# Attention scores as three fp32r products in place of one f32 product, in a whole two-block model

## The chip, the cores and the metric

The kernel runs on one core of one Trainium2 chip: TensorE (PE in the profile) multiplies, its weight loads are listed apart as PEld; VectorE (DVE), ScalarE (ACT) and GpSimd (POOL) do the rest, and SyncE (SP) issues most transfers. The metric is device time in microseconds (us) for one execution. Engines run their own instructions in order, and wait for each other by semaphores.

## The reference, cut to what matters

One batch of 512 tokens, 1024 wide, goes through two blocks. Block one: a hybrid attention (8 heads of a sparse kind with three branches: compressed keys, selected keys, a window; 8 heads of a block kind), then a mixture of 32 experts. Block two: a convolution of 31 taps beside a forgetting attention of 16 heads, then a layer that gathers experts (PEER). All is f32. With 512 tokens, the selections cover all visible keys, so that each branch is a causal softmax with a bias.

```python
qn = rms_norm(_heads(q_n, NSA_HEADS), nsa_q_gain)          # 8 heads of 64
kc = rms_norm(_compress(k_cmp, ...), k_gain)               # 31 compressed keys
ks, kw = rms_norm(k_slc, k_gain), rms_norm(k_win, k_gain)  # 2 groups of 64
s = einsum("bghcd,bgcmd->bghcm", qn, ks) * scale - sl * dist   # selected; window alike
o = gates[0] * softmax(s_cmp) @ vc + gates[1] * softmax(s_slc) @ vs + gates[2] * softmax(s_win) @ vw
# 8 heads of the block kind
qm, km = rms_norm(_heads(q_m, 8), moba_q_gain), rms_norm(_heads(k_m, 8), moba_k_gain)
o = softmax(qm @ km.T * scale - sl * dist) @ vm
# block two, forgetting attention; c = cumsum(log_sigmoid(f))
s = einsum("bhqd,bhkd->bhqk", q, k) / 8 + c[..., :, None] - c[:, :, None, :]
o = softmax(where(causal, s, NEG_2)) @ v
```

## The kernel before

Activations lie transposed, features on partitions. A value that goes into a wide product is kept as two fp32r parts, the high part a rounded copy and the low part what is left (`split`, L121 to L128: ACT copies, DVE subtracts), and a product is three matmuls, high by high, high by low, low by high (`mm3`, L130). Weights come in chunks of 128 columns through `stream` (L184): SP loads them into three raw buffers, ACT makes `sh` (L202), and DVE, or in the second attention POOL (`self.low`), makes `sl` (L203), two chunks ahead of use. The attention scores alone are f32 matmuls of 64 rows by head (`attend`, L986).

`attend` (L972 to L1055) runs both attentions. A unit is a pair of heads, a block of 128 queries and all keys up to it, 128 to 512. The first attention has 48 units (per head pair j four query blocks by two branches: 32 units; then four pairs of the block kind: 16), the second 32 (eight pairs by four blocks). Turn t issues, in this order: the two heads' scores of unit t (L986, with the forget term L988 added in the second attention), the maximum on DVE (`aw`, L1000) and the exponential on ACT (`ap`, L1003); the division of unit t-1 (one head on ACT, one on DVE, L1009 to L1017); the transposes of unit t-2 (L1025) with copies (`apt`, L1029 DVE, L1031 ACT); the products with values of t-3 (L1040). Each head has one bank of scores.

Between two turns the caller puts work that doesn't belong to the unit. In the first attention: one entry of the list `self.later`, then a chunk of the projection, eight steps of `mm3` in PSUM bank `acc`. Chunks come in the order key, query, value of each pair, numbered from 0 (0 and 1 are `vs`, `vw`). A finished query or key chunk goes through `head_norm` (L240): ACT writes the square and a copy times -0.5 at once (L247, L248); the rest, put on `self.later`, is a matmul that sums the squares by head (L252), three steps on ACT (Ln, Exp, Square: L254, L255, L258) and three on DVE (L259, L260, L261, the last writes the normalised heads `qn`, `qm`, `km`). A finished value chunk is copied by ACT (`vT`, L232) and later turned. The list is emptied in full (`flush`) ahead of units 0, 8, 16, 24, 32, 36, 40 and 44, where a new head pair begins and DVE makes its two bias tables (`bias`, L599).

In the second attention each turn puts six taps of the convolution on DVE (L1514, 240 in all, 12 in each fourth turn) and a chunk: per head pair j the query and the key chunk, copied out of PSUM by ACT (L1538), values, and two chunks of the convolution's input (`sg`, `zc` L1508). A finished pair is split by ACT and DVE (`evac`, L1565, L1566).

What sets the order is this program order; the framework puts in the waits and gives out the buffers by name.

Of the kernel before, what the change touches and what calls it, by code (L numbers as in the profile page):

```python
# [20 lines left out]
S, D = 512, 1024  # L21
# [22 lines left out]
class Model:  # L44
# [183 lines left out]
    def turned(self, dst, ps, pool, mm, after=None):  # L228

        nc = self.nc  # L230
        t = pool.tile([128, S], F, name="vT", bufs=1)
# [11 lines left out]
    def head_norm(self, pool, mm, ps, gain, out, n=512, bufs=1):  # L243

        nc = self.nc
        sq = pool.tile([128, 512], F, name="sq", bufs=2)
# [3 lines left out]
        def rest():  # L250
# [10 lines left out]
            nc.vector.scalar_tensor_tensor(out, out, gain, r, op0=OP.mult, op1=OP.mult)  # L261

# [53 lines left out]
    def block1(self):  # L316
# [6 lines left out]
        qn, qm, km = ([pa.tile([128, S], F, name=f"{n}{j}") for j in range(4)] for n in ("qn", "qm", "km"))  # L323
# [5 lines left out]
        ks, kw = (pb.tile([128, S], F, name=n) for n in ("ks", "kw"))  # L329
        vs, vw, *vm = (pb.tile([128, TB, 128], F, name=f"v{i}") for i in range(6))  # L330
        gat = pb.tile([128, TB, 24], F, name="gat")
        kcT = pb.tile([128, 32], F, name="kcT")
# [139 lines left out]

        def tile_T():
            if pre:
                return pre.pop(0)
            ps = tile()
            self.zT(ps, next(w1), hT)
            return ps
# [45 lines left out]
        def compressed():  # L524
# [3 lines left out]
            self.head_norm(ea, mm, p2, self.col("nkg", 1), kcT, 32, bufs=2)  # L528
# [22 lines left out]
        for i, t in enumerate((ks, kw)):  # L551
            self.head_norm(ea, mm, tile_T(), self.col("nkg", 1), t, bufs=2)
        self.head_norm(ea, mm, tile_T(), qg[:, 0:1], qn[0], bufs=2)
# [11 lines left out]
        def work():  # L565
            take = banks("acc", "ot")
            for i in range(-2, 15):
# [12 lines left out]
                j, r = (i + 1, 0) if i < 3 else ((i - 3) // 3, i % 3 + 1)  # L580
                if r == 0:
                    self.head_norm(at, mm, ps, qg[:, 0:1], qn[j])
                elif r == 1:
                    self.head_norm(at, mm, ps, qg[:, 1:2], qm[j])
                elif r == 2:
                    self.head_norm(at, mm, ps, self.col("mkg", 1), km[j])
# [8 lines left out]
        def biases(key, heads):  # L595
            self.flush()
            bias[key] = at.tile([128, 2, 512], F, name="bias", bufs=2)
# [4 lines left out]
        def begin(j):  # L602

            biases(j, (j, j + 4))
            w = at.tile([128, 2, TB, 32], F, name="cw", bufs=2)
            for i in range(2):
                ps = psa.tile([128, TB, 32], F, name=f"sc{i}")
                for qb in range(TB):
                    nc.tensor.matmul(ps[:, qb], qn[j][half(i), qb * 128:qb * 128 + 128], kcT[half(i)],
                                     start=True, stop=True)  # L610
                cb = at.tile([128, TB, 32], F, name="cb", bufs=2)
                nc.vector.scalar_tensor_tensor(cb, dc, -(2.0 ** -(j + 4 * i + 1)), neg, op0=OP.mult, op1=OP.add)
                nc.vector.tensor_tensor(w[:, i], ps, cb, op=OP.add)
# [23 lines left out]
        def evac(j, ot):  # L637

            def f():
                m, n = divmod(j, 4)  # L640
                hi = pa.tile([128, S], FR, name=("qn", "qm")[m] + str(n))
# [1515 lines left out]


COLS = {}


def ktile(a):

# [102 lines left out]
```

## Time and profile before

| | us |
|---|---|
| median of three runs | 3699.92 (3698.37 to 3701.18) |
| the profiled execution | 3701.02 |
| its span, first to last instruction | 3699.3 |
| first attention, about 101 to 392 | 291 |
| experts, weights streaming, about 600 to 1640 | 1040 |
| second attention, about 1797 to 2145 | 348 |

Over the span PE is busy 94%, DVE 81%, ACT 55%, POOL 31%. The shares are means over stages with different limits, so they are read stage by stage: the busy time of an engine in a stretch says whether it can be the limit there; the chain of waits follows the work that ended last back in time and says which engine it ran over; a row in order of time gives a start, a duration, and in brackets how long the engine was idle before and what ended that. A row with x2 joins neighbours of a kind. Matmuls are pipelined: the distance of two starts says more than the duration of one.

### The profile page before, as it was taken

What the parts mean: (1) busy time and instruction counts of PE and PEld (TensorE: products, weight loads), DVE (VectorE), ACT (ScalarE), POOL (GpSimd) and SP (SyncE); (2) the same over time, 40 slices, a digit from 0 to 9 for tenths busy, and PEclk for the clock granted to TensorE, in tenths of its full rate; (3) what the DMA queues carried; (4) which work ended last, traced back from release to release, by engine and by line L of the source; (5) the groups of instructions that cost most, each with busy time, mean ns of one, the idle gap of its engine ahead of it and who ended that gap; (6) DMA issues with size and microseconds to landing.
All of it is one profiled execution on the core that took longest, in us unless ns stands there. A gap on an engine that the chain in (4) does not pass through costs nothing.

```text
span 3699.3 us, 48276 instructions
## 1 busy us (share of the span) xinstructions
PE 3485.2 (94%) x16965; PEld 2802.7 (76%) x16966; DVE 2986.2 (81%) x4775; ACT 2051.2 (55%) x3226; POOL 1135.5 (31%) x745
## 2 busy tenths in 40 slices
PE   7998869999999999998999999997999999999998
PEld 5665657777777777776776778787889999999876
DVE  5676389999999999998799955599977777777777
ACT  4455468888888888886433343422763333333333
POOL 0567021111110111100133310266964444433342
PEclk9889979999999999999999999998999999999999
DMA  5233469999999999994212123221478888888886
GB/s 202 97 104 111 151 239 351 358 352 361 356 356 354 354 357 358 353 358 157 76 57 66 60 82 101 97 92 58 195 268 312 296 301 300 300 295 293 302 274 221
DMA packets 230092, 866.84 MB, mean 234 GB/s; under 512 B 21922, under 2 KB 73250, under 8 KB 179156
## 3 DMA queue, kind: packets, MB, share of 16 engines
q1 hardware_dynamic: 131680, 641.33, 47.4%
q0 software_dynamic: 47104, 171.14, 14.5%
q10 hardware_dynamic: 51060, 51.23, 4.1%
q8 instruction: 136, 2.23, 0.2%
q14 instruction: 112, 0.92, 0.1%
HBM read 815.31 MB, written 48.30 MB: 233 GB/s over the span
## 4 chain that ended last, share of the span: by engine, by line
PE 33%; DVE 13%; POOL 3%; ACT 2%; DMA 1%; issue 1%; ACTq 0%; DVEq 0%; POOLq 0%
PE out L2058 13%; DVE conv L1514 6%; PE a L135 4%; PE a L133 4%; PE a L134 4%; PE mm L133 2%; PE mm L134 2%; PE mm L135 2%; POOL o L1956 2%; DMA vr<-in_peer_vt 1%; DVE eq L1845 1%; POOL ul L1733 1%; DVE ex L1853 1%; DVE t L1933 1%; DVE aw L1000 1%
## 5 line engine op out<-in xcount | busy, mean ns | idle before, releaser
L1130 DVE TENSOR_TENSOR elo<-raw,ehi 128x1024 fp32r<-128x1024 f32 x384 | 449.7, 1219 | 17.6 <-ACT ehi L1128 17.6
L1128 ACT ACTIVATE ehi<-raw 128x1024 fp32r<-128x1024 f32 x384 | 395.7, 1056 | 71.3 <-PE y L1231 36.1
L135 PE MATMUL a<-hT,ul 128*128 128x384 f32 x1024 | 347.3, 339 | 21.5 <-POOL ul L1733 20.8
L133 PE MATMUL a<-hT,uh 128*128 128x384 f32 x1024 | 346.7, 339 | 0.9 <-ACT uh L1732 0.9
L134 PE MATMUL a<-hT,uh 128*128 128x384 f32 x1024 | 345.1, 337 | 0.0
L1231 PE MATMUL u<-ehi,xgTh 128*128 128x512 f32 x1024 | 342.8, 416 | 0.5 <-ACT xgTh L1172 0.5
L1231 PE MATMUL u<-elo,xgTh 128*128 128x512 f32 x1024 | 322.4, 396 | 0.8 <-DVE elo L1130 0.8
L1231 PE MATMUL u<-ehi,xgTl 128*128 128x512 f32 x1024 | 322.6, 396 | 0.0
L2058 PE MATMUL out<-vh,ah 128*128 128x512 f32 x768 | 304.0, 396 | 3.3 <-ACT ah L125 3.1
L2058 PE MATMUL out<-vl,ah 128*128 128x512 f32 x768 | 302.5, 394 | 0.0
L1130 DVE TENSOR_TENSOR elo<-hT,ehi 128x1024 fp32r<-128x1024 f32 x252 | 296.3, 1236 | 0.6 <-ACT ehi L1128 0.6
L2010 ACT ACTIVATE vh<-vr 128x1024 fp32r<-128x1024 f32 x128 | 135.8, 1061 | 283.5 <-issue 184.9
L1128 ACT ACTIVATE ehi<-hT 128x1024 fp32r<-128x1024 f32 x256 | 256.4, 1049 | 60.1 <-PE y L1231 51.6
L2011 DVE TENSOR_TENSOR vl<-vr,vh 128x1024 fp32r<-128x1024 f32 x128 | 156.8, 1225 | 145.1 <-ACT vh L2010 142.9
L2023 POOL DMA_INDIRECT gu<-in_peer_u,pidx x128 | 196.4, 1535 | 249.4 <-DVE gu L2032 226.5
L1197 POOL DMA_INDIRECT x_d<-ysb,row x31 | 71.2, 2298 | 648.3 <-DVE ysb L1284 627.3
L1514 DVE SCALAR_TENSOR_TENSOR conv<-zc,taps,conv 128x512 f32<-128x512 f32 x240 | 263.4, 1099 | 7.2
L2023 POOL DMA_INDIRECT gu<-in_peer_v,pidx x128 | 180.7, 1412 | 288.1 <-DVE h L2039 262.6
L133 PE MATMUL mm<-hT,sh 128*128 128x512 f32 x648 | 264.1, 408 | 0.1
L135 PE MATMUL mm<-hT,sl 128*128 128x512 f32 x648 | 257.3, 397 | 0.0
L203 POOL TENSOR_TENSOR sl<-sraw,sh 128x1024 fp32r<-128x1024 f32 x60 | 155.0, 2596 | 311.1 <-ACT sh L202 296.0
L2058 PE MATMUL out<-vh,al 128*128 128x512 f32 x768 | 241.3, 395 | 0.0
(572 smaller groups left out, 8633.5 us busy)
## 6 DMA issues: line engine op xcount, KB each, us to landing
raw<-in_exp_w SPq DMA_DIRECT2D x192, 1024.0 KB
hT<-in_exp_w SPq DMA_DIRECT2D x128, 1024.0 KB
sraw<-in_w SPq DMA_DIRECT2D x128, 512.0 KB
xt<-in_exp_w SPq DMA_DIRECT2D x64, 1024.0 KB
ur<-in_peer_ut SPq DMA_DIRECT2D x128, 512.0 KB
vr<-in_peer_vt SPq DMA_DIRECT2D x126, 512.0 KB
adaw<-in_ada_w SPq DMA_DIRECT2D x96, 256.0 KB
G_d<-G ACTq DMA_DIRECT2D x12, 2048.0 KB
```

The source lines that it names most:

```text
L133: nc.tensor.matmul(ps, lh, rh, start=start, stop=False)
L134: nc.tensor.matmul(ps, lh, rl, start=False, stop=False)
L135: nc.tensor.matmul(ps, ll, rh, start=False, stop=stop)
L203: (self.low or nc.vector).tensor_tensor(spl[i][1], r, spl[i][0].bitcast(F), op=OP.subtract)
L1128: nc.scalar.activation(hi, src, AF.Copy)
L1130: eng.tensor_tensor(lo, src, hi.bitcast(F), op=OP.subtract)
L1231: nc.tensor.matmul(dst[n], x, w[:, n * 512:n * 512 + 512], start=ch >= 8 and k == 0 and x is xh and w is hi, stop=k == KC - 1 and w is lo)
L1514: nc.vector.scalar_tensor_tensor(o, z[:, w:w + S], taps[:, 31 * j + w:31 * j + w + 1], o, op0=OP.mult, op1=OP.add)
L2010: nc.scalar.activation(hi, r, AF.Copy)
L2011: nc.vector.tensor_tensor(lo, r, hi.bitcast(F), op=OP.subtract)
L2023: nc.gpsimd.indirect_dma_start(out=gu[i], out_offset=None, in_=A["peer_u" if i < 128 else "peer_v"], in_offset=bass.IndirectOffsetOnAxis(a ...
L2058: nc.tensor.matmul(out[tb][n], x, w[:, n * 512:n * 512 + 512], start=i == 0 and x is ah and w is hi, stop=i == 127 and x is al)
```

## The change

Scores become three fp32r products per head, q high by k high, q low by k high, q high by k low, with the two heads' products in turns, and the forget terms behind them. For this all normalised queries and keys, and q and k of the second attention, are kept as two parts. `head_norm` writes into a buffer `hn` and hands it to `split`; in the second attention ACT writes the high part straight from PSUM and DVE subtracts it. The order of the chunks comes from the table `WORK` (r: 0 query of the sparse kind, 1 query, 2 key, 3 value of the block kind): queries come first, values and keys in turns after, and keys are held for two pairs only. `ks` and `kw` lie in two of the buffers of x, which is read again at unit 32. The compressed keys become a block with zeros that takes both heads in one full-height f32 product. Several pools have a buffer less.

```diff
-    def head_norm(self, pool, mm, ps, gain, out, n=512, bufs=1):
+    def head_norm(self, pool, mm, ps, gain, done, n=512, bufs=1):
+        out = pool.tile([128, 512], F, name="hn", bufs=bufs)[:, :n]
...
             nc.vector.scalar_tensor_tensor(out, out, gain, r, op0=OP.mult, op1=OP.mult)
+            done(out)
...
-        kcT = pb.tile([128, 32], F, name="kcT")
+        kcT = pb.tile([128, 2, 32], F, name="kcT")
+        nc.vector.memset(kcT, 0.0)
+        def own_columns(src):
+            for i in range(2):
+                nc.vector.tensor_copy(kcT[64 * i:64 * i + 64, i], src[64 * i:64 * i + 64])
...
+        nc.scalar.dma_start(self.x_d[S:, :], self.xt[0])
+        ks, kw = ([t[:, i] for i in range(2)] for t in (
+            self.per.tile([128, 4, S], FR, name="xt", bufs=2) for _ in range(2)))
+        parts = lambda t: lambda src: self.split(*t, src)
+        def moba_keys(j):
+            def f(src):
+                km[j] = [pk.tile([128, S], FR, name=f"km{i}", bufs=2) for i in range(2)]
+                self.split(*km[j], src)
+            return f
...
-                j, r = (i + 1, 0) if i < 3 else ((i - 3) // 3, i % 3 + 1)
+                r, j = WORK[i]
...
-                    self.head_norm(at, mm, ps, self.col("mkg", 1), km[j])
+                    self.head_norm(at, mm, ps, self.col("mkg", 1), moba_keys(j))
...
-            bias[key] = at.tile([128, 2, 512], F, name="bias", bufs=2)
+            bias[key] = at.tile([128, 2, 512], F, name="bias")
...
+            ps = psa.tile([128, TB, 2, 32], F, name="sc0")
+            for qb in range(TB):
+                for a in range(2):
+                    nc.tensor.matmul(ps[:, qb], qn[j][a][:, qb * 128:qb * 128 + 128].bitcast(F), kcT,
+                                     start=a == 0, stop=a == 1)
...
+        def three(keys):
+            def f(q, i, qs, n):
+                (qh, ql), (kh, kl) = (t[half(i), qs] for t in q), (t[half(i), :n] for t in keys())
+                return (qh, kh), (ql, kh), (qh, kl)
+            return f
...
+            if t == 8 * TB:
+                self.x_tiles()
+                for tb in range(TB):
+                    nc.sync.dma_start(self.xt[tb], A["x"][tb * 128:(tb + 1) * 128, :])
...
-            for i in range(2):
-                ps = psp.tile([128, 512], F, name=f"sc{i}", bufs=scb)
-                extra = u.get("add")
-                nc.tensor.matmul(ps[:, :n], u["q"][i], u["k"][i], start=True, stop=extra is None)
-                if extra is not None:
-                    nc.tensor.matmul(ps[:, :n], *extra(i), start=False, stop=True)
+            for a, pairs in enumerate(zip(*(u["qk"](i) for i in range(2)))):
+                for ps, (q, k) in zip(s["ps"], pairs):
+                    nc.tensor.matmul(ps[:, :n], q, k, start=a == 0, stop=extra is None and a == 2)
+            if extra is not None:
+                for i in range(2):
+                    nc.tensor.matmul(s["ps"][i][:, :n], *extra(i), start=False, stop=True)
...
-                for t, sc in ((q, 0.125), (k, 1.0)):
-                    nc.scalar.activation(t[j], tile_T(), AF.Copy, scale=sc)
-                    yield
+                qh, ql, kh, kl = qk[j]
+                ps = tile_T()
+                nc.scalar.activation(qh, ps, AF.Copy, scale=0.125)
+                nc.vector.scalar_tensor_tensor(ql, ps, 0.125, qh.bitcast(F), op0=OP.mult, op1=OP.subtract)
+                yield
+                self.split(kh, kl, tile_T())
+                yield
...
+WORK = [(0, 1), (0, 2), (0, 3), (1, 0), (1, 1), (1, 2), (1, 3), (3, 0), (2, 0), (3, 1), (2, 1), (3, 2), (2, 2),
+        (3, 3), (2, 3)]
```

ACT in the first attention, where a finished head norm is taken from the list between two units; before (`rr`, `sq` are steps of the norm, `sh` the next weight chunk's high part, `ap` the next unit's exponentials):

```order
L254 ACTIVATE rr<-mm,eps 128x512
L255 ACTIVATE rr<-rr 128x512
L258 ACTIVATE sq<-rr 128x512
L202 ACTIVATE sh<-sraw 128x1024
L1003 ACTIVATE ap_1108,asum<-aw_1105,am_1106 128x384
L1003 ACTIVATE ap_1113,asum<-aw_1110,am_1111 128x384
```

and now:

```order
L255 ACTIVATE rr<-mm,eps 128x512
L256 ACTIVATE rr<-rr 128x512
L259 ACTIVATE sq<-rr 128x512
L125 ACTIVATE qn_0_108<-hn 128x512
L202 ACTIVATE sh<-sraw 128x1024
L1036 ACTIVATE ap_1153,asum<-aw_1150,am_1151 128x384
```

The copy that makes the high part (L125) stands between the norm's last step on ACT and the weight chunk's high part.

DVE at the same place, before (`qn` is the normalised query, `sl` the weight chunk's low part, `aw` the next unit's maximum):

```order
L1029 COPY apt_1064<-pt_1062 128x128
L259 SCALAR_TENSOR_TENSOR sq<-mm,sq 128x512
L260 SCALAR_TENSOR_TENSOR rr<-sq,rr 128x512
L261 SCALAR_TENSOR_TENSOR qn_106<-qn_106,qg,rr 128x512
L203 TENSOR_TENSOR sl<-sraw,sh 128x1024
L1000 ISA aw_1105,am_1106<-sc_1100,bias 128x384
```

and now:

```order
L1062 COPY apt_1103<-pt_1101 128x128
L260 SCALAR_TENSOR_TENSOR sq<-mm,sq 128x512
L261 SCALAR_TENSOR_TENSOR rr<-sq,rr 128x512
L262 SCALAR_TENSOR_TENSOR hn<-hn,qg,rr 128x512
L128 TENSOR_TENSOR qn_1_109<-hn,qn_0_108 128x512
L203 TENSOR_TENSOR sl<-sraw,sh 128x1024
L1033 ISA aw_1150,am_1151<-sc_1141,bias 128x384
```

One subtraction (L128) stands between the norm's third step and the weight chunk's low part.

DVE in the second attention, from the end of a head pair over a turn with twelve taps, before (`k<-ot` is the pair's split, `conv` the taps):

```order
L1015 TENSOR_SCALAR ap_16791<-ap_16791,asum 128x256
L1029 COPY apt_16848<-pt_16846 128x128
L1566 TENSOR_TENSOR k_16859<-ot,q_16858 128x512
L1514 SCALAR_TENSOR_TENSOR conv_16085<-zc,taps,conv_16085 128x512 x12
L1000 ISA aw_16945,am_16946<-sc_16938,maskneg 128x512
L1000 ISA am_16946 128x1
L1000 ISA aw_16950,am_16951<-sc_16941,maskneg 128x512
```

and now:

```order
L1062 COPY apt_17128<-pt_17126 128x128
L1604 TENSOR_TENSOR k_17139<-ot,q_17138 128x512
L1548 SCALAR_TENSOR_TENSOR conv_16325<-zc,taps,conv_16325 128x512 x6
L1574 SCALAR_TENSOR_TENSOR k_17149<-mm,q_17148 128x512
L1548 SCALAR_TENSOR_TENSOR conv_16325<-zc,taps,conv_16325 128x512 x6
L128 TENSOR_TENSOR kl<-mm,kh 128x512
L1033 ISA aw_17235,am_17236<-sc_17224,maskneg 128x512
L1033 ISA am_17236 128x1
```

The low part of the query stands behind the sixth tap, that of the key behind the twelfth, ahead of the next unit's maximum.

DVE ahead of unit 44, the last head pair of the first attention, before:

```order
L1009 RECIPROCAL asum<-asum 128x2
L1015 TENSOR_SCALAR ap_3398<-ap_3398,asum 128x384
L1029 COPY apt_3460<-pt_3457 128x256
L599 SCALAR_TENSOR_TENSOR bias<-dist,maskneg 128x512 x2
L1000 ISA aw_3487,am_3488<-sc_3482,bias 128x128
L1000 ISA am_3488 128x1
```

and now:

```order
L1042 RECIPROCAL asum<-asum 128x2
L1048 TENSOR_SCALAR ap_3624<-ap_3624,asum 128x384
L1062 COPY apt_3690<-pt_3687 128x256
L260 SCALAR_TENSOR_TENSOR sq<-mm,sq 128x512
L261 SCALAR_TENSOR_TENSOR rr<-sq,rr 128x512
L262 SCALAR_TENSOR_TENSOR hn<-hn,colv,rr 128x512
L128 TENSOR_TENSOR km_3715<-hn,km_3714 128x512
L621 SCALAR_TENSOR_TENSOR bias<-dist,maskneg 128x512 x2
L1033 ISA aw_3730,am_3731<-sc_3721,bias 128x128
```

The three steps of the last key chunk's norm and its subtraction now stand ahead of the bias tables and the unit's maximum; before, a value chunk was due there, with nothing on DVE.

## Rows read from the trace of the kernel before

**Rows 1.** Three stages: us; busy PE, PEld, DVE, ACT, POOL; clock; DMA share; GB/s.
```profile
101.00:392.00 291.00, 262.66 (x1549) 176.05 (x1549) 190.33 (x505) 158.69 (x390) 179.72 (x123) 0.92 0.30 101
600.00:1640.00 1040.00, 1000.09 (x4440) 774.85 (x4439) 983.40 (x1032) 865.76 (x1083) 110.82 (x55) 1.00 0.98 356
1797.00:2145.00 348.00, 340.77 (x1644) 242.63 (x1646) 329.09 (x492) 125.47 (x275) 116.95 (x55) 0.98 0.19 63
```

**Rows 2.** Chain of waits, second attention, shares by line.
```profile
by line: DVE conv L1514 64.0%; DVE aw L1000 5.6%; PE mm L133 3.0%; DVE apt L1029 2.9%; PE mm L134 2.8%; PE mm L135 2.7%; issue 2.6%; DVE ap L1015 2.5%; ACT ap L1003 2.3%; DVE zc L1508 1.6%; PE sc L986 1.6%; DVE conv L1510 1.4%; DVE L L1559 
```

**Rows 3.** Waits of engines, second attention: total us, times, longest.
```profile
DVE k L1566 <- ACT q L1565: 9.2, 7, 1.3
...
PE sc L986 <- DVE am L1000: 5.8, 5, 1.8
```

**Rows 4.** DVE, part of one head pair: start us, us, what, idle before.
```profile
1938.14 0.69 DVE L1566 TENSOR_TENSOR k<-ot,q 128x512 fp32r<-128x512 f32 x1 [1.34 <-ACT q L1565]
1938.74 13.45 DVE L1514 SCALAR_TENSOR_TENSOR conv<-zc,taps,conv 128x512 f32<-128x512 f32 x12
...
1974.48 0.74 DVE L1514 SCALAR_TENSOR_TENSOR conv<-zc,taps,conv 128x512 f32<-128x512 f32 x1
```

**Rows 5.** POOL in the same stretch.
```profile
1939.13 5.43 POOL L203 TENSOR_TENSOR sl<-sraw,sh 128x1024 fp32r<-128x1024 f32 x2 [6.08 <-ACT sh L202]
```

**Rows 6.** DVE, second attention, all taps: busy us, mean ns, idle.
```profile
L1514 DVE SCALAR_TENSOR_TENSOR conv<-zc,taps,conv 128x512 f32<-128x512 f32 x235 | 259.7, 1106 | 7.0
```

**Rows 7.** POOL, second attention, all such splits: busy us, mean ns, idle.
```profile
L203 POOL TENSOR_TENSOR sl<-sraw,sh 128x1024 fp32r<-128x1024 f32 x41 | 109.1, 2672 | 196.9 <-ACT sh L202 185.1 <-PE pt L1025 11.7
```

**Rows 8.** ACT in the stretch of Rows 4: two chunks leave PSUM.
```profile
1939.47 0.60 ACT L1538 ACTIVATE q<-mm 128x512 f32<-128x512 f32 x1 [0.41 <-PE mm L135]
...
1945.07 0.60 ACT L1538 ACTIVATE k<-mm 128x512 f32<-128x512 f32 x1 [4.05 <-PE mm L135]
```

**Rows 9.** PE, scores of one unit, second attention, 512 keys.
```profile
1989.70 1.12 PE L986 MATMUL sc<-k,q 64*128 64x512 f32 x2
...
1991.07 1.12 PE L986 MATMUL sc<-k,q 64*128 64x512 f32 x2
```

**Rows 10.** ACT, first attention, a head norm between two units.
```profile
229.87 0.63 ACT L258 ACTIVATE sq<-rr 128x512 f32<-128x512 f32 x1
230.40 1.04 ACT L202 ACTIVATE sh<-sraw 128x1024 fp32r<-128x1024 f32 x1
```

**Rows 11.** DVE in the same stretch.
```profile
230.53 0.69 DVE L259 SCALAR_TENSOR_TENSOR sq<-mm,sq 128x512 f32<-128x512 f32 x1 [1.72 <-ACT sq L258]
...
231.98 0.75 DVE L261 SCALAR_TENSOR_TENSOR qm<-qm,qg,rr 128x512 f32<-128x512 f32 x1
232.65 2.32 DVE L203 TENSOR_TENSOR sl<-sraw,sh 128x1024 fp32r<-128x1024 f32 x1
234.90 0.54 DVE L1000 CUSTOM_DVE_ANT_0 aw<-sc,bias 128x384 f32<-128x384 f32 x1
```

**Rows 12.** ACT, the flush ahead of unit 32, both ends of its chain.
```profile
299.55 0.58 ACT L247 ACTIVATE sq<-acc 128x512 f32<-128x512 f32 x1
...
308.37 0.40 ACT L1003 ACTIVATE ap<-aw,am 128x128 f32<-128x128 f32 x1 [5.01 <-DVE am L1000]
```

**Rows 13.** ACT, the flush ahead of unit 44.
```profile
368.11 0.58 ACT L232 ACTIVATE vT<-acc 128x512 f32<-128x512 f32 x1
...
370.28 0.40 ACT L1003 ACTIVATE ap<-aw,am 128x128 f32<-128x128 f32 x1 [0.25 <-DVE am L1000]
```

**Rows 14.** Ahead of the first unit, weight loads of PE.
```profile
93.43 0.32 PEld L542 LDWEIGHTS mm<-ident,gT 32*128 32x128 f32 x4 [3.25 <-ACT gT L537]
```

**Rows 15.** PE, one unit of the first attention, 512 keys.
```profile
321.07 0.39 PE L134 MATMUL acc<-hT,sh 128*128 128x512 f32 x1
321.30 0.40 PE L135 MATMUL acc<-hT,sl 128*128 128x512 f32 x1
321.63 1.13 PE L986 MATMUL sc<-km,qm 64*128 64x512 f32 x4
```

## What I expect, and why

> **What bounds the kernel now.** I read the profiled execution stage by stage: busy time by stretch, then the chain of waits inside a stretch, then single engines in order of time. Its time is 3701.0 us; the median of the three runs is 3699.9, so sums made on the profile are moved by -1.1 at the end. 0.2% of it, about what a measurement of this kernel can tell from no change, is 7.4 us.
>
> The first attention lasts 291 us with no engine full: PE 263, DVE 190, ACT 159 [rows 1]. The reader should see a loop limited by hand-overs: scores, maximum, exponential, norm, transpose, product, with a chunk of the projection filling PE between. The MoE behind it has its DMA engines at 0.98 for 1040 us at 356 GB/s [rows 1]: its weights start when the first attention frees its buffers, so what is lost ahead of it arrives at the end in full, and nothing is caught up.
>
> The second attention (348 us) has PE busy 341 and DVE 329 [rows 1]. Busy time alone would name PE. The chain of waits there names DVE: 64% of it is the taps of the convolution, and PE's matmuls, scores included, make some 10% [rows 2]. The waits between engines agree: PE's scores wait 5.8 us for DVE's maximum, which has to empty the bank; DVE's only repeated wait is 9.2 us, 7 times 1.3, for ACT's copy of a finished head pair, and no maximum waits for PE [rows 3]. PE is thus close behind DVE but behind it. Work added to DVE here is paid, and work taken from PE is not.
>
> **The change part by part.**
>
> Second attention, splits. The copies of query and key chunk stay on ACT, and DVE subtracts: two more instructions per head pair, in seven of the eight pairs inside the loop (the first pair's lie ahead of it), 14 in all. The nearest instruction, with one operand in PSUM and the same shape, took 0.69 and was followed after about 0.72 (two steps from 230.53 to 231.98) [rows 11]. 14 x 0.72 = +10.1. No wait comes with them: ACT has emptied the query chunk at 1940.1 and the key chunk at 1945.7 [rows 8], and the subtractions stand behind the sixth tap (about 1947) and the twelfth (1952.2) [rows 4]. If they were as quick as the distance behind the subtraction of a head pair's end, 0.60 [rows 4], they cost 8; with 0.3 more each for a late ACT, 14.
>
> Second attention, scores. A head takes 1.12 for its two f32 instructions (and 0.39 for the forget term), and the second head starts 1.37 behind the first [rows 9]: they run one after another, since the forget term, which uses both halves of the array, lies between. In the changed order the two heads' products stand side by side and the forget terms come last. That shortens PE's part of a unit, but only the 1.6% of the chain that is scores (some 5.6 us of 348) [rows 2] can give something back: -1 (from 0 to -3).
>
> Here the splits also meet POOL, which makes the low part of the weights. A tap alone takes 0.74 [rows 4]; twelve taps beside two POOL splits (5.43) [rows 5] took 13.45 [rows 4]. 12 x 0.74 = 8.9, so each POOL split cost DVE some 2.3. Over the stage the mean tap is 1.106 [rows 6], 235 x 0.366 = 86 us above the plain one, and there are 41 POOL splits [rows 7]: 2.1 each. If an instruction of another kind than a tap stood beside the POOL split, that could be less; this is the rival on the fast side, below. The Trainium skill (SBUF — State Buffer, Who interferes with whom) says that a DVE instruction with two SBUF inputs contends with a GpSimd instruction that reads SBUF, and that one with at most one SBUF input does not; by that rule the taps are held up, as the rows above show, and a subtraction whose source is PSUM would not be, which no row of this case shows. It gives no other sum unless the POOL splits begin at other places.
>
> First attention, norms. A head norm now ends with a hi copy on ACT and a subtraction on DVE. Eleven norms lie inside the loop. Take one of before: ACT makes its last step at 229.87 and then at once the weight chunk's high part, 230.40 to 231.44 [rows 10]; DVE does three steps from 230.53, the last at 231.98 for 0.75, then the low part of the weights without idle, 232.65, and the next maximum at 234.90 [rows 11]. In the changed order ACT's hi copy waits for the third DVE step (232.7) and takes 0.58, as ACT's pass over the same shape does [rows 12], and the weight chunk's high part, queued behind it, ends at 234.3; DVE's subtraction fits in between, and the low part starts at 234.3 instead of 232.65: +1.7. Queued behind the waiting hi copy are the weight chunk's high part and the next exponentials; DVE waits for both. Of the eleven, two fall into flushes that held none (next paragraph), one into the flush ahead of unit 32, where only the hi copy and the subtraction are added, 0.6 + 0.7 = 1.3, and eight into pops between units. Two of these lie where PE's work chunk ends last; I take half for them. 6 x 1.7 + 2 x 0.85 + 1.3 = +13. If a late chunk of PE hides half of the pops, it is 5; if each also delays the next unit's exponentials by the subtraction (0.72 x 9), 19.
>
> First attention, the new order of chunks. The last chunk, due ahead of unit 44, was values (a copy and a turn) and is now keys with a norm that the unit's scores wait for. Ahead of unit 32 such a flush takes from 299.55 to the first exponential at 308.37: 8.8 [rows 12]; ahead of unit 44 it took from 368.11 to 370.28: 2.2 [rows 13]. With the split (1.3) it becomes 10.1: +7.9. In turn chunk 15 is values now: a pop with a norm (1.7 idle, 2.2 of steps [rows 11]: some 4) goes away. At unit 16 the flush takes a query norm instead of a turn, which is not needed until later, and chunk 9 turns from a norm into values: nil. A point off because the last units have no chunk left to wait behind: +3 (from -1, if all slack is used, to +8).
>
> Ahead of the first unit. Three norms are split there and their hi copies stand in ACT's queue ahead of the gates. PE already waits 3.25 there for ACT's gT [rows 14]. Now the hi copy of the last of these norms, ahead of gT, waits for DVE's three steps (2.2) and takes 0.6, 2.8 at a stretch; the two before cost some 1.2 for copy and subtraction with half of it beside other work: +4 (2 to 6).
>
> First attention, scores. Four f32 instructions of both heads take 1.13 [rows 15], as long as two of one head [rows 9]: pairs on the two halves of the array already run together. A full-height fp32r product goes on after 0.23 (321.07 to 321.30) [rows 15]. No row shows one of 64 rows. If pairs run together, three take 0.7, 0.4 less at 512 keys, 0.2 in the mean of 48 units: -10 if all of it counts; if they run one after another, 6 x 0.23 = 1.4, 0.3 more, up to +14. Nearest to these are the f32 pairs of rows 15, which run together; and most of a unit's distance is hand-over. I take -2, with -4 and +14 as ends. The compressed scores go from 64-row pairs to full-height f32 with two terms: +1 for four times.
>
> At nothing: x is read again at unit 32 by four transfers on SP's queue, ahead of the later weight loads, and wait there only for unit 31's scores, already issued; the three raw buffers of the stream cover them, and DMA is busy 0.30 there [rows 1]. The earlier write of x_d takes its place in ACT's queue instead of a later one. Bias, softmax rows and the convolution's inputs lose a buffer each: their writer is DVE itself, or the reader has been done for a whole unit (some 9 us).
>
> Sum: +10.1 - 1 + 13 + 3 + 4 - 2 + 1 = +28. 3701.0 + 28 - 1.1 = **3728 us**, 0.8% slower.
>
> **The rivals.**
>
> Serial products: if the 64-row fp32r products of both heads don't run together, first attention pays up to 16 more than my -2: 3744, with PE's gaps perhaps at the lower clock (its mean is 0.92 there, between levels of 1.2 and 2.4 GHz [rows 1]).
>
> Absorbed: the pops' delays lie behind PE's chunk, and the flush ahead of unit 44 is eaten by its slack: 5 - 1 + 2 in place of 13 + 3 + 4, thus 3714; with splits at 6, 3710.
>
> No change: if also DVE in the second attention has slack at the pairs' ends (9.2 us of waits [rows 3]) and the 14 splits fall into it, +1 remains: 3701 to 3705. Against it: that wait comes behind ACT's copy at a place where no split stands.
>
> Faster: the subtractions, which read PSUM, move the taps against POOL, and are not held up by it as taps are. Where a POOL split then runs under a subtraction or a maximum and not under a tap, DVE saves 2.1. With three of the five per head pair, 21 x 2.1 = 44 is saved, and the time is 3728 - 44 = 3684. It decides from 28 / 2.1 = 13 of the 41 on. Against: the POOL split starts when ACT's high part is ready, at 1939.13, half a us into the taps [rows 4, 5], and the new subtractions stand six taps later.
>
> **How the numbers follow.** Forecast, 3715 to 3742: 0.55. Serial products or a lower clock, 3742 to 3755: 0.13. Absorbed, 3707 to 3715: 0.15. No change, 3695 to 3707: 0.10. Faster, 3684: 0.07. The range leaves out the fast side and the highest part of the serial case: 3706 to 3750, some 0.8. Slower by over 0.2% (above 3707.3): 0.82; within: 0.11; faster: 0.07.
>
> **What would show it.** In the second attention the chain should still be DVE's, its busy time up by 10, the taps' mean near 1.1, PE's score instructions shorter and PE waiting more; a tap mean under 1.0 would be the rival on the fast side. The first attention should be some 15 longer and the part ahead of it 4, with the weight split's high part late behind the hi copy at each pop, and a gap of 8 to 10 ahead of unit 44. The MoE should keep its length and start later. Wrong would be: the second attention shorter, or a first attention as long as before.

## The result, and the profile after

The changed kernel takes 3739.8 us (median of four runs, 3738.3 to 3742.9) against 3699.2 for the kernel before on the same chip: ratio 1.0108, interval 1.0093 to 1.0123, 40.6 us slower. The forecast was 3728 with a range from 3706 to 3750. The sign and the range held; the first attention cost twice what was forecast, and where it went is the subject of what follows.

The two profiled executions are laid side by side at landmarks, the starts of the first maximum on DVE of a unit:

| stretch | before | after | difference | forecast |
|---|---|---|---|---|
| start to unit 0 of the first attention | 108.7 | 110.7 | +2.0 | +4 |
| unit 0 to unit 47 | 272.1 | 302.1 | +30.0 | +15 |
| unit 47 to unit 0 of the second attention | 1403.9 | 1407.5 | +3.6 | 0 |
| unit 0 to unit 31 of the second | 341.0 | 347.4 | +6.4 | +9 |
| unit 31 to the end | 1573.6 | 1571.6 | -2.0 | 0 |

The first, the third and the last row move from one execution to the next. In the three profiles with the first attention as before, unit 0 comes at 105.6 to 108.7; in the ten with the changed scheme and its splits, at 110.0 to 114.3. Over all fourteen profiles the third row lies between 1402.0 and 1407.6 and the last between 1570.7 and 1575.3, so the 3.6 and the -2.0 are not firm. The other two rows are: the second is 271.3 to 274.0 in the three profiles with the first attention as before and 301.5 to 304.2 in the three with the changed one untouched, and the fourth is 346.7 to 347.6 in the nine whose second attention is split and gets the weights' low part from POOL, against 341.0 in the one profile before.

Stages of the changed kernel, columns as in [rows 1]; the first line goes from unit 0 to unit 47:

```profile
110.70:412.80 302.10, 253.79 (x1546) 177.23 (x1544) 185.73 (x488) 158.79 (x387) 168.00 (x113) 0.88 0.31 102
636.00:1676.00 1040.00, 999.99 (x4439) 774.85 (x4440) 983.17 (x1033) 866.05 (x1083) 110.94 (x55) 1.00 0.98 356
1833.00:2187.50 354.50, 327.39 (x1706) 246.87 (x1707) 336.06 (x506) 125.29 (x275) 117.20 (x53) 0.95 0.19 61
```

The experts have kept their busy times and their 356 GB/s and only start later. In the second attention DVE has gained 7 and PE lost 13 us of busy time, and the stage is longer. In the first, PE's mean granted clock has fallen.

The norm that answers to [rows 10, 11], the same query chunk, on ACT and then on DVE of the changed kernel:

```profile
247.66 0.63 ACT L259 ACTIVATE sq<-rr 128x512 f32<-128x512 f32 x1
250.56 0.63 ACT L125 ACTIVATE qm<-hn 128x512 fp32r<-128x512 f32 x1 [2.27 <-DVE hn L262]
251.10 1.04 ACT L202 ACTIVATE sh<-sraw 128x1024 fp32r<-128x1024 f32 x1
```

```profile
248.33 0.69 DVE L260 SCALAR_TENSOR_TENSOR sq<-mm,sq 128x512 f32<-128x512 f32 x1 [1.71 <-ACT sq L259]
...
249.78 0.75 DVE L262 SCALAR_TENSOR_TENSOR hn<-hn,qg,rr 128x512 f32<-128x512 f32 x1
251.23 1.01 DVE L128 TENSOR_TENSOR qm<-hn,qm 128x512 fp32r<-128x512 f32 x1 [0.70 <-ACT qm L125]
252.18 1.23 DVE L203 TENSOR_TENSOR sl<-sraw,sh 128x1024 fp32r<-128x1024 f32 x1
253.32 0.55 DVE L1033 CUSTOM_DVE_ANT_0 aw<-sc,bias 128x384 f32<-128x384 f32 x1
```

The high part of the weights starts 3.4 after the norm's last step on ACT, where it was 0.5; their low part starts 2.4 behind the start of DVE's third step, where it was 0.67. That is the wait of 1.7 that the forecast had priced, to the tenth. The maximum behind it moved less in this pair: it starts 3.54 after the start of the third step, where it was 2.92, since the low part took 2.32 in [rows 11] and takes 1.23 here. In [rows 11] a sum on POOL ran beside it, here none does. Low parts of over 1.5 come 5 times among 31 before and 4 times now, so this is an accident of the place.

The flush ahead of unit 16, ACT of the changed kernel:

```profile
214.25 0.60 ACT L248 ACTIVATE sq<-acc 128x512 f32<-128x512 f32 x1 [2.39 <-PE acc L135]
...
221.34 0.63 ACT L125 ACTIVATE qm<-hn 128x512 fp32r<-128x512 f32 x1 [3.26 <-DVE hn L262]
227.03 0.42 ACT L641 ACTIVATE cw<-cw 128x256 f32<-128x256 f32 x1 [5.06 <-DVE cw L640]
229.84 0.40 ACT L1036 ACTIVATE ap<-aw,am 128x128 f32<-128x128 f32 x1 [2.40 <-DVE am L1033]
```

A norm, its split and then the bias tables and the compressed softmax stand in one row: 15.6 us from the square to the unit's first exponential, and 20.9 from unit 15 to unit 16, where it was 11.1.

The second attention, DVE of the changed kernel, at the place of [rows 4], then two of its waits and its chain by line:

```profile
1976.13 0.69 DVE L1604 TENSOR_TENSOR k<-ot,q 128x512 fp32r<-128x512 f32 x1 [1.27 <-ACT q L1603]
1976.74 8.71 DVE L1548 SCALAR_TENSOR_TENSOR conv<-zc,taps,conv 128x512 f32<-128x512 f32 x6
1985.37 0.68 DVE L1574 SCALAR_TENSOR_TENSOR k<-mm,q 128x512 fp32r<-128x512 f32 x1
1985.97 4.68 DVE L1548 SCALAR_TENSOR_TENSOR conv<-zc,taps,conv 128x512 f32<-128x512 f32 x6
1990.57 0.68 DVE L128 TENSOR_TENSOR kl<-mm,kh 128x512 fp32r<-128x512 f32 x1
1991.17 0.68 DVE L1033 CUSTOM_DVE_ANT_0 aw<-sc,maskneg 128x512 f32<-128x512 f32 x1
```

```profile
PE sc L1019 <- DVE am L1033: 14.4, 15, 2.2
...
DVE k L1604 <- ACT q L1603: 8.8, 7, 1.3
```

```profile
by line: DVE conv L1548 52.8%; issue 5.5%; DVE aw L1033 5.3%; PE mm L133 5.0%; PE mm L134 4.7%; PE mm L135 4.5%; ACT ap L1036 2.9%; DVE apt L1062 2.3%; DVE ap L1048 1.8%; PE pt L1058 1.5%; PE ot L1073 1.4%; DVE k L1604 1.4%; ACT ap L1050 1.
```

The two subtractions stand without idle time between taps and maximum, and the taps are still over half of the chain; PE's wait for that maximum has grown from 5.8 [rows 3] to 14.4. What PE saves it spends waiting.

### The profile page after: what moved, and what is told of

The parts are those of the page before. It is cut to its first block, busy times and chain, and to the rows that moved or that the text cites. A ratio compares the mean times of both kernels' runs of the same rounds, so it can differ in the third digit from the quotient of the medians.

```text
span 3739.3 us, 48683 instructions
## 1 busy us (share of the span) xinstructions
PE 3475.0 (93%) x17125; PEld 2816.5 (75%) x17126; DVE 3002.0 (80%) x4808; ACT 2059.2 (55%) x3240; POOL 1138.5 (30%) x745
## 3 DMA queue, kind: packets, MB, share of 16 engines
q0 software_dynamic: 47104, 171.14, 14.4%
## 4 chain that ended last, share of the span: by engine, by line
PE 33%; DVE 12%; POOL 3%; ACT 2%; issue 1%; DMA 1%; ACTq 0%; DVEq 0%; SPq 0%; POOLq 0%
PE out L2096 13%; DVE conv L1548 5%; PE a L135 4%; PE a L133 4%; PE a L134 4%; PE mm L133 3%; PE mm L134 3%; PE mm L135 3%; POOL o L1994 2%; DVE eq L1883 1%; POOL ul L1771 1%; DMA vr<-in_peer_vt 1%; DVE ex L1891 1%; DVE t L1971 1%; DVE aw L1033 1%
## 5 line engine op out<-in xcount | busy, mean ns | idle before, releaser
L135 PE MATMUL a<-hT,ul 128*128 128x384 f32 x1024 | 346.7, 339 | 22.2 <-POOL ul L1771 21.6
```

The lines of the kernel that those rows point to most:

```text
L135: nc.tensor.matmul(ps, ll, rh, start=False, stop=stop)
```

## The experiments

Each is one kernel; times are medians, with a median of 3698 to 3700 for the kernel before beside every group of runs (its single runs lie between 3689 and 3707). "Units 0 to 47" is the distance of the table above, from the profile of that kernel.

**e1. The order of the chunks.**

```diff
-WORK = [(0, 1), (0, 2), (0, 3), (1, 0), (1, 1), (1, 2), (1, 3), (3, 0), (2, 0), (3, 1), (2, 1), (3, 2), (2, 2),
-        (3, 3), (2, 3)]
+WORK = [(0, 1), (0, 2), (0, 3), (1, 0), (1, 1), (3, 0), (1, 2), (1, 3), (3, 1), (2, 0), (2, 1), (3, 2), (2, 2),
+        (2, 3), (3, 3)]
```

> The changed kernel with another table WORK: queries first, but values stand again at the places where they stood before (chunks 7, 10, 13 and 16), norms at all others. Theory (the order costs: norms now stand ahead of units 16, 26 and 44, where the next unit waits for them): the steps from unit 15 to 16, 25 to 26 and 43 to 44 fall back by 9, 7 and 6 us, the places that had become values give back some 8, so 14 to 16 less, about 3725. Rival (the splits cost wherever they stand, the order nothing): 3740 within 3. Rival (six score products in place of two delay each unit): 3740 too, with unit distances unchanged.

Measured 3732.9: 7 less, not 15. The three steps fell as expected: against the kernel before, 15 to 16 is +3.3 (it was +9.8), 25 to 26 is -0.2 (+8.0) and 43 to 44 is +1.5 (+6.8). But the places that are norms again took more back than their 8: the steps at units 13, 23, 29 and 42 alone rose by 2.1, 4.4, 4.9 and 4.7. Units 0 to 47 last 297.4, against 272.1 before with norms and values in the same places. So the order is worth 5 to 7, and 25 us are left for splits and products.

**e2. The split behind the weights' parts.** In a turn the split is issued after the next chunk's first step; flushes keep theirs.

```diff
-            done(out)
+            if self.late is None:
+                done(out)
+            else:
+                self.late.append(lambda: done(out))
...
                 next(W)
                 n += 1
+                for f in self.late:
+                    f()
```

> The changed kernel with the split of a norm that is taken between two units of the first attention issued one step later, behind the weight chunk's high part on ACT and its low part on DVE; splits in flushes stay. Theory (the weight chunk's high part waits behind the norm's high part): the low part of the weights starts 1.6 earlier at eight places, the subtraction then stands behind it and takes 0.6 back, so 8 less, about 3732 (3728 to 3736). Rival (these places have cover, the loss is in flushes alone): 3740 within 2.

Measured 3732.6, units 0 to 47 in 294.0 in place of 302.1: 7 less in the time and 8 in the stretch, as expected. The wait of ACT for the norm is a real part of the price.

**e3. Both parts on DVE.**

```diff
-        parts = lambda t: lambda src: self.split(*t, src)
+        parts = lambda t: lambda src: self.split(*t, src, hi_eng="v")
```

> The changed kernel with both parts of a norm's split made on DVE in the first attention, so that ACT never waits for the norm. Theory: ACT's high part of the weights comes early, but DVE gets 0.6 more at each of 11 norms and the low part of the weights starts only 0.3 earlier; 2 to 4 less, about 3737. Rival (the hand-over from DVE to ACT and back is the whole price): 11 x 1.3 less, about 3726.

Measured 3733.6; units 0 to 47 in 299.4, 2.7 less. The stretch agrees with the theory, and so does its profiled execution, the slowest of four with 3737.7; the median lies between theory and rival. The hand-over alone is not the price.

**e4. The first attention alone.**

```diff
-                nc.scalar.activation(qh, ps, AF.Copy, scale=0.125)
-                nc.vector.scalar_tensor_tensor(ql, ps, 0.125, qh.bitcast(F), op0=OP.mult, op1=OP.subtract)
+                for x, sc in zip(qk[j], (0.125, 1.0)):
+                    nc.scalar.activation(x, tile_T(), AF.Copy, scale=sc)
```

> The changed kernel with the second attention's scores as before: q and k whole in f32, one product per head, no splits; its smaller buffers and the heads' products in turns stay. Theory (DVE bounds this stage): the step of each double turn falls by 1.0, 7 in all, 5 to 7 less at the end, about 3734. Rival (PE bounds it, and its score products became cheaper by 14 us of busy time): 3745 or more.

Measured 3732.3, 7.5 less. Each of the seven double turns is 1.0 longer in the changed kernel than before; here none is (0.07 at most), and units 0 to 31 of the second attention last 339.3. The f32 products cost nothing at all. Nor do they keep PE much busier: the score instructions between units 0 and 31, before, in the changed kernel and in e4 (busy PE first, behind the length):

```profile
1784.70:2125.70 341.00, 66.16 (x189) 18.64 (x126) 27.41 (x63) 0.00 (x0) 0.97 0.18 61
1820.30:2167.70 347.40, 40.10 (x249) 16.63 (x186) 27.29 (x62) 0.00 (x0) 0.95 0.18 60
1819.20:2158.50 339.30, 41.35 (x186) 12.48 (x124) 27.35 (x63) 0.00 (x0) 0.95 0.19 61
```

Of the 26 us that PE saves on scores here, 25 come from the new order (both heads' products first, the forget terms last), and 1 from the three fp32r products. A unit at 512 keys in e4, 1.50 from its first start to that of the transposes:

```profile
1978.73 1.13 PE L1019 MATMUL sc<-k,q 64*128 64x512 f32 x4
1979.79 0.60 PE L1022 MATMUL sc<-R,L 96*128 96x512 bf16 x2
1980.23 0.60 PE L1058 MATMUL pt<-ident,ap 128*128 128x128 f32 x4
```

It was 2.65 for the unit of [rows 9], and is 1.34 in the changed kernel.

**e5. f32 scores beside the splits.**

```diff
-                return (qh, kh), (ql, kh), (qh, kl)
+                return (qh.bitcast(F), kh.bitcast(F)),
```

> The changed kernel with the splits and the order of chunks as they are, but in the first attention the scores are one f32 product per head, made from the high parts (the low parts are made and not used, so the scores lose their low bits). Theory (the loss lies in the splits and the order, the products are worth little): two f32 products take 1.13 at 512 keys against 0.97 for the six, some 0.1 a unit in the mean; +2, about 3742 (3739 to 3746). Rival (six products with their weight loads hold up the units): 3730 or less.

Measured 3735.1, units 0 to 47 in 296.8, 5 less: neither. The six products seemed to cost some 5. e9 seems to contradict it, so e5 by itself decides nothing on the products; that the clock makes both possible (e12) is argued, not shown. For the splits it gives a second price: e5 and the kernel before both have f32 scores, and between units 0 and 47 they differ by 24.7. Less the 5 of the order (e1), some 20 are left for the splits.

**e6. One head after the other.**

```diff
-            for a, pairs in enumerate(zip(*(u["qk"](i) for i in range(2)))):
-                for ps, (q, k) in zip(s["ps"], pairs):
+            for i, ps in enumerate(s["ps"]):
+                for a, (q, k) in enumerate(u["qk"](i)):
```

> The changed kernel with the three products of one head issued before those of the other, in both attentions. Theory (pairs on the two halves of the array run together, and the second attention waits for DVE anyway): in the first attention six products one after another take 1.4 instead of 0.97 at 512 keys, 0.27 in the mean, 48 units, about half of it hidden: +6, about 3746, all before the experts; the second attention unchanged. Rival (turns are worth nothing, loads and products overlap in any order): 3740 within 2.

Measured 3740.4: no change, the rival. The six products take the same time either way; PE, one unit at 512 keys, 0.91 to the next start:

```profile
344.50 0.97 PE L1019 MATMUL sc<-km,qm 64*128 64x512 f32 x6
345.41 0.66 PE L1058 MATMUL pt<-ident,ap 128*128 128x128 f32 x4
```

Putting the heads "in turns" is worth nothing in this kernel. In the f32 scheme of the second attention the forget term between the heads kept them apart [rows 9], and e4 shows f32 products side by side once it stands last; it stands last in both versions here.

**e7, e8. The weights' low part on DVE in the second attention,** in the changed kernel and in the kernel before.

```diff
-        self.low = nc.gpsimd
         for t, _ in enumerate(self.attend(units, at, psa, scb=1, awb=1)):
```

> The changed kernel with the low part of the weights made by DVE instead of POOL in the second attention. Theory (a POOL split blocks a tap for 2.1, a DVE split takes 1.22): DVE is relieved by 41 x 0.9 = 36, and PE, busy 327 of the stage's 354, becomes the bound: 20 less, about 3720 (3712 to 3730). Rival (DVE then waits for ACT's high part, which stands behind exponentials): 3740 or more.

> The kernel before with the low part of the weights made by DVE instead of POOL in the second attention. Theory: the same relief of DVE, but PE is busy 341 of 348 with the f32 scores and bounds the stage at once: 4 to 7 less, about 3694. The stage is then longer than that of the changed kernel with the same edit by some 10. Rival (PE's busy time has slack inside): 20 or more less, 3680.

Measured 3709.9 and 3686.8, 30 and 13 less than without the edit; units 0 to 31 in 317.0 and 327.9. Both gained more than their theories had (20, and 4 to 7). e7, the stage and then two DVE groups:

```profile
1834.00:2160.00 326.00, 314.24 (x1724) 237.89 (x1725) 306.39 (x551) 126.18 (x277) 11.11 (x12) 0.99 0.20 65
```

```profile
L1548 DVE SCALAR_TENSOR_TENSOR conv<-zc,taps,conv 128x512 f32<-128x512 f32 x240 | 182.4, 762 | 6.9
L203 DVE TENSOR_TENSOR sl<-sraw,sh 128x1024 fp32r<-128x1024 f32 x40 | 49.3, 1246 | 0.0
```

The taps' mean falls from 1.106 [rows 6] to 0.762: 77 us of DVE time come back for 49 spent. e8, the stage and its chain:

```profile
1791.00:2127.00 336.00, 335.26 (x1644) 239.80 (x1644) 298.00 (x537) 126.58 (x275) 10.45 (x12) 0.99 0.19 63
```

```profile
by line: PE mm L133 23.9%; PE mm L134 22.5%; PE mm L135 22.4%; PE sc L986 13.6%; PE ot L1040 6.4%; PE pt L1025 5.3%; PE sc L988 4.4%; PE mm L237 0.9%; DVE zc L1508 0.2%; DVE L L1559 0.2%; DVE conv L1510 0.2%; DVE aw L1000 0.1%; issue 0.0%; 
```

With DVE relieved, PE is busy 335.3 of 336 and the f32 scores are 13.6% of the chain: here the cheaper scores count, 10.9 us between e8 and e7. By e4 it is their order that makes nearly all of the saving on PE; no run has f32 products in the new order with the low part on DVE, so how much of the 10.9 they would give without any split is not shown.

**e9. No splits in the first attention.** e1, with DVE's last step writing the rounded high part, and one buffer of zeros for all low parts.

```diff
-            nc.vector.scalar_tensor_tensor(out, out, gain, r, op0=OP.mult, op1=OP.mult)
-            done(out)
+            nc.vector.scalar_tensor_tensor(done.whole(), out, gain, r, op0=OP.mult, op1=OP.mult)
...
-                (qh, ql), (kh, kl) = (t[half(i), qs] for t in q), (t[half(i), :n] for t in keys())
+                (qh, ql), (kh, kl) = (t[half(i), qs] for t in (q[0], zero)), (t[half(i), :n] for t in (keys()[0], zero))
```

> The kernel of e1 (values in their old places) without the splits in the first attention: the norm's last step on DVE writes the high part itself, rounded, and the low parts of queries and keys are one buffer of zeros, so all six products still run but the scores lose their low bits. Theory (with the order restored, the 25 us that remain between units 0 and 47 are the splits on ACT and DVE): 20 less than e1, about 3712. Rival (the six products, or PE at its lower clock for other reasons, carry most of it): 3728 to 3733.

Measured 3699.0, 34 less than e1. Units 0 to 47 take 262.8, 9.3 less than before the change. The theory had the right culprit and too small a sum. The smaller buffers, the second read of x and the new block of compressed keys are all still in e9, so none of them explains the loss. Units 0 to 47 in e1, and then in e9:

```profile
114.10:411.50 297.40, 261.98 (x1558) 183.11 (x1556) 182.97 (x487) 159.72 (x387) 167.01 (x113) 0.87 0.31 103
```

```profile
110.00:372.80 262.80, 235.19 (x1543) 163.91 (x1541) 178.21 (x476) 152.01 (x376) 171.96 (x113) 0.96 0.35 117
```

PE does the same products, and is busy 27 us less, at a mean clock of 0.96 instead of 0.87 (levels are 1.2 and 2.4 GHz). Its idle time differs by only 8. Two of the three products of a head read zeros in e9, and no run separates what that does to the clock. Most of the rise seems to need no zeros: the three profiles with the first attention as before, which have no splits and read no zeros, show 0.93 to 0.95 over the same units. PE of e9, the scores of a unit at 512 keys, shows pairs of 64-row products 0.23 to 0.34 apart, so the two heads run together:

```profile
191.22 0.50 PE L1033 MATMUL sc<-xt,qn 64*128 64x512 f32 x2
191.56 0.40 PE L1033 MATMUL sc<-xt,zero 64*128 64x512 f32 x2
191.79 0.40 PE L1033 MATMUL sc<-zero,qn 64*128 64x512 f32 x2
```

**e10. e1 and e2 together,** the table of e1 and the edit of e2.

```diff
-WORK = [(0, 1), (0, 2), (0, 3), (1, 0), (1, 1), (1, 2), (1, 3), (3, 0), (2, 0), (3, 1), (2, 1), (3, 2), (2, 2),
+WORK = [(0, 1), (0, 2), (0, 3), (1, 0), (1, 1), (3, 0), (1, 2), (1, 3), (3, 1), (2, 0), (2, 1), (3, 2), (2, 2),
...
-            done(out)
+                self.late.append(lambda: done(out))
```

> The changed kernel with the edits of e1 and e2 together: values in their old places, and a split taken between units issued behind the weight chunk's parts. Theory (two separate costs, 7 each as measured alone): 14 less than the changed kernel, about 3726. Rival (both take away the same wait): 3732 or more.

Measured 3725.2: 14.6 less than the changed kernel, units 0 to 47 in 286.2. The two costs add, as the theory has it.

**e11. The second attention alone, with the weights' low part on DVE.** The kernel before with the second attention of e7.

```diff
+                nc.vector.scalar_tensor_tensor(ql, ps, 0.125, qh.bitcast(F), op0=OP.mult, op1=OP.subtract)
...
-        self.low = nc.gpsimd
```

> The kernel before with the change in the second attention alone, and the low part of the weights made by DVE there. Theory (with DVE relieved, PE bounds the stage, and the cheaper score products count): the stage is 24 shorter than before, as in e7, about 3676 (3670 to 3682), below e8 by 11. Rival (the 24 of e7 hung on the later start or on the smaller buffers): 3687 or more.

Measured 3675.8 (3673.0 to 3677.6), ratio to the kernel before 0.9939 (0.9922 to 0.9955). Units 0 to 31 take 318.5, 22.5 less than before. It beats both kernels, and e8 by 11; of its 24 us below the kernel before, e8 alone has 13.

**e12. Products that lead to nothing.** e1, with six more products ahead of the eight chunks that start behind a popped norm.

```diff
+                for _ in range(6 if self.fill else 0):
+                    nc.tensor.matmul(ps, w[0][:, 0], hT[0][0], start=True, stop=True)
```

> The kernel of e1 (values in their old places, all splits in) with six products more on PE, each overwritten by the first one of the chunk that follows, ahead of the eight chunks that start behind a norm taken between two units: 8 x 6 x 0.23 = 11 us of PE work that leads to nothing, put where PE would later stand idle for DVE's maximum. In e1 PE was busy 262 us between units 0 and 47 at a mean granted clock of 0.87, in e9 235 at 0.96 for the same products. Theory (a good part of what a split costs is PE's clock, which falls behind gaps): the filler lies in the gaps, the mean clock rises above 0.89 and the time stays or falls, 3720 to 3734. Rival (the clock is a by-product, the work adds to the path): 5 to 11 more than e1, 3738 to 3744, at the same clock.

Measured 3724.8 (3718.6 to 3728.6 in six runs), 8 less than e1, with 11 us of work more:

```profile
114.30:401.60 287.30, 257.78 (x1599) 181.40 (x1597) 184.97 (x488) 159.38 (x387) 167.02 (x113) 0.92 0.32 107
```

The trace has 41 PE instructions more in that stretch than in e1, and PE is busy 4 us and idle 6 us less. The clock is no by-product: it is part of the price.

## Why the prediction was right, and where it was wrong

The time stayed in the range because the range was wide: one stretch alone missed its forecast by 15.

**Second attention: right.** DVE bounds it, PE's saving is worth nothing there, and the splits are paid. Their size was somewhat high: a subtraction takes 0.60 to the next start, not 0.72, and a tap hands over to it after 0.67, where to another tap it takes 0.78, so a double turn is 1.0 longer and not 1.45 (e4 shows the seven steps gone). The working also named what shortens PE's part, the order of the products; e4 confirms it, with 25 of 26 us.

**The splits of the norms: right mechanism, the term that was mis-sized.** "6 x 1.7 + 2 x 0.85 + 1.3 = +13" had the wait right, 1.7 on DVE. Between e1 and e9 the stretch differs by 34.6, with f32 scores by some 20 (e5), so the splits cost 20 to 35 and not 13. The step that failed was to price a wait by its own length and to hold PE's speed fixed. PE waits more (idle 23 us between units 0 and 47 before, 35 in e1), its mean clock falls (0.92 before [rows 1], 0.87 in e1), and the products behind take longer than they did. In the changed kernel, two units at 512 keys, the second behind an idle time of 2.62:

```profile
199.39 0.97 PE L1019 MATMUL sc<-xt,qn 64*128 64x512 f32 x6
200.28 0.88 PE L1058 MATMUL pt<-ident,ap 128*128 128x128 f32 x6
...
206.63 2.26 PE L1019 MATMUL sc<-xt,qn 64*128 64x512 f32 x6 [2.62 <-DVE am L1033]
209.07 1.54 PE L1058 MATMUL pt<-ident,ap 128*128 128x128 f32 x6 [0.17 <-ACT apt L1064]
```

The same six products take 2.26 instead of 0.97, the same six transposes 1.54 instead of 0.88. The granted clock is 1.00 from 199.0 to 206.0 and 0.50 from 207.2 to 214.0. The forecast had the lower clock only in a rival, hung on serial products, which they are not (e6, e9).

**The order of the chunks: near in sum, wrong in its places.** +3 was forecast; e1 gives 5 in the stretch and 7 in the time. At unit 44 the working was right (+6.8 against 7.9). At unit 16 "nil" was wrong: that the query is not needed until later does not help, since a flush puts its three DVE steps and its split ahead of the bias tables of the pair that begins, and the step grew by 9.8. The swap at unit 26 (+8.0) was overlooked. Both were balanced by places that became values (-2.9, -3.5, -3.0 at units 23, 29, 42).

**Scores in the first attention: the saving was sized too large, and its worth stays open.** The working put three pairs at 0.7 at 512 keys; they take 0.90, against 1.06 from start to start for the four f32 instructions of [rows 15]. e9 against before gives -9.3, e5 against the changed kernel the other sign, with six products 5 slower. The products alone can't give 9.3 by their own time, and the mean clock differs too (0.96 against 0.93), so what they are worth is not shown. That turns make no difference (e6) was not among the rivals.

**Two side sums are off.** With half of the pops hidden, the norms cost some 7 and not 5. And the +14 for serial products takes the 0.3 of 512 keys for all 48 units; scaled as the -10 was, it is 7, and the serial rival moves from 3744 to some 3737, inside the forecast's own range. Neither enters the 3728.

**The start:** 2 in the profiled pair, some 6 in the mean of the profiles (three with the first attention as before, ten as changed), for a forecast of 4.

**The rival on the fast side** was rightly held small for this change: the POOL splits still meet the taps (40 of them, 2.69 each). Its condition never arose: all 14 new subtractions run with no POOL instruction beside them, 0.68 each. The prediction said that no row of the case shows a subtraction with a PSUM source that isn't held up. The trace of the changed kernel has none beside POOL either, but it has a near relative: the maxima of 384 keys, which read scores from PSUM and a mask from SBUF, take 0.55 whether one of POOL's sums of convolution rows (L1553, L1555) covers more than 60% of them (4) or not (12), while taps take 2.30 with POOL beside them (54) against 0.75 (181). No maximum stands beside a POOL split. This agrees with the Trainium skill (SBUF — State Buffer, Who interferes with whom): two SBUF inputs contend, one does not outside the 2-port modes.

Left open: which part of the 34.6 is waiting, which is the clock, and which comes from the zeros of e9. PE's busy time puts 27 on the slower products and 8 on idle time, but the two feed each other; e12 gives 8 to 10 back by filling gaps alone. Why e5 was 5 faster than the changed kernel is not settled either; a phase of the units in which fewer of them meet the lower clock (0.89 against 0.88 over the stretch) is only argued.

## What to carry to other kernels

A cheaper product needs its operands in parts, and the parts are made on the engines that may already set the pace: ask first which engine waits for which, and price the preparation there. Look first for the same saving without the parts: in the second attention the order of the products alone, in f32, gave 25 of the 26 us that PE saves on scores (e4). In the first attention, a loop bound by hand-overs, small waits put ahead of a busy TensorE cost more than their length, and the products behind them ran at a lower clock; read the granted clock of the stretch beside each wait that a change adds. And before taking work off one engine, look at what its helper does to it: here 13 of the 24 us of the fastest kernel (e11) came from taking a task back from POOL (e8).

## What the runs showed of the hardware that was not expected

- f32 products of two heads, 64 rows each, took 2.65 for a unit at 512 keys with a product of 96 rows between the heads, and 1.50 with those products last (before, e4).
- 11 us of useless products made the kernel 8 us faster (e12): mean granted clock 0.92 in place of 0.87 between units 0 and 47.
- Two heads' fp32r products on the two halves of the array overlap as well when one head's three are issued first: 0.91 for six at 512 keys in e6, 0.90 in the changed kernel.
- A DVE instruction of 1.25 us was cheaper than the same work on POOL beside it: 41 POOL splits stretch the taps by some 77 us, 40 DVE splits cost 49 (e7).
